# One half of a modulation bank computed at a layer boundary instead of inside the layer before, with a scratch tile and a modulation step rearranged

## The chip, the cores and the metric

The kernel runs on one core of a Trainium2 chip. The metric is the device time of one execution in microseconds (us); lower is better. Three runs of the kernel before gave 1622.14, 1630.13 and 1632.17 us, with a median of 1630.13 us.

## The reference, cut to what matters

The program is a trunk of two layers over 256 context and 256 latent tokens of width 1024, followed by a final norm. Each layer has six modulation vectors, each 1024 wide, worked out from a conditioning vector:

```python
mod = silu(c) @ w_ada[l] + b_ada[l]        # 6 x 1024 columns, mods 0 to 5
h   = rms_norm(x, norm1[l]) * (1 + scale) + shift
x   = x + gate * w_out(merge(conv(h), retention(h), mla(h)))   # one in-projection for the three
h2  = rms_norm(x, norm2[l]) * (1 + scale2) + shift2
x   = x + gate2 * moe(h2)                  # 16 experts, top 2 in groups
```

Everything is float32. The kernel stores the modulations in three banks of 2048 columns: bank 0 holds mods 0 and 1 (shift and scale of the first norm), bank 1 mods 2 and 3, bank 2 mods 4 and 5. In bank 1 of layer 1, mod 2 is the gate after the mixers and mod 3 the shift of the second norm.

## The kernel before, in words

**Numbers.** A float32 operand is split into a rounded part and a rest (`hi`, `lo`), and a product is three matmuls: hi by hi, lo by hi, hi by lo. In the trace the rounded weight is `whi` or `ehi` (made by ACT), its rest `wlo` or `elo` (made by DVE, L383 and L1095). The three matmuls are lines L185 to L187 in the projections, L192, L193 and L195 in the experts, and L1472, L1473 and L1475 in the last quarters of the last expert.

**Modulation banks (class `Ada`, L233).** A bank is computed in eight k-steps of 128 rows of `w_ada`. A step (L276) multiplies `silu(c)` by four column groups of 512 and sends the result of group g to partitions 32g to 32g+31 of one PSUM tile, `psa`. `add` (L287) adds the bias, and `finish` writes the bank to DRAM, from where `mod_row` reads it as rows. In layer 0 the banks (0,1), (0,2), (1,0) and (1,1), written as (layer, bank), stand in the list `todo`. `fill` takes one step of it behind a projection of layer 0, and `load` brings the step's weights, 128x2048 or 1 MB, into the single buffer `adaw`. Bank (1,2) is read through the stream of expert weights and multiplied where PE waits for the router, around 620 us.

**Expert weights.** `pieces` lists all weight pieces of a layer's experts, 512 KB each. `prefetch` (L1058) starts the load of the next piece on SP's queue as soon as a buffer is offered; `weights` (L1081) takes the next piece, makes `ehi` and `elo`, and gives the buffer back; `raw_piece` (L1075) does the same without making them. So a load that reuses a buffer waits for the last reader of the piece in it.

**The boundary.** `last_expert` (L1477) runs expert 15 of layer 0: its up projections (`ps<-ehi,xh` and so on), its transposed activations (L1444), its gate product `gg` (L1453), its down projection, first into the two tiles `py`, then in four quarters of 256 columns into `ps`. In `add`, PE scatters the result back to the tokens (L1491, `ps<-yg,ohT`), DVE multiplies it by a gate into `eth` (L1503) and adds that to `resid` (L1505), and ACT squares the new `resid` into a scratch tile, also a buffer of the tag `eth` (L1507), summing the squares. From these sums DVE makes the norm's factor (L201 to L209) and the normed rows `xn` (L564) of layer 1. Before these quarters stands a branch (L1562) on a flag that tells of overflowing experts; it isn't taken here, but every engine passes it.

Layer 1 then transposes `xn` (PE, L571), modulates it (`modulate`, L419: DVE makes `t` with scale and shift, L424; ACT rounds it to `hh`, L427; DVE makes `hl`, L428) and starts its in-projection (L185) while the rest is modulated.

**Order.** The order of the source is not the order of the engines: the framework's scheduler places each instruction in its engine's queue, and each queue then runs in order. `tc.issue_after` holds an instruction behind another one.

The lines that the change and the steps of the prediction touch:

Of the kernel before, what the change touches and what calls it, by code (L numbers as in the profile page):

```python
# [10 lines left out]
F32 = mybir.dt.float32  # L11
# [97 lines left out]
def tile_hybrid(ctx, tc, x, c, ctxt, c_ctx, w_ada, b_ada, norm1, norm2, w_in, ret_decay, ret_gn, w_ret_o,  # L109
# [18 lines left out]
    def nm(s):  # L128
        uid[0] += 1
        return f"{s}_{uid[0]}"  # L130
# [102 lines left out]
    class Ada:  # L233

        def __init__(self, l, b, pool, bufs, tps, alloc):
            self.l, self.b, self.pool, self.bufs, self.tps, self.alloc = l, b, pool, bufs, tps, alloc
            self.ps = None
            self.w = {}  # L240
            self.loaded = {}

        def prep(self):
            l, b = self.l, self.b
            self.bias = [self.alloc() for _ in range(1 if b == 1 else 2)]
            for t in self.bias:
                G.memset(t, 0.0)
            for g in range(4):
                r = b_ada[l, b * 2048 + g * 512:b * 2048 + (g + 1) * 512]
                nc.gpsimd.dma_start(self.bias[0][32 * g:32 * g + 2, :], r.partition_broadcast(2))  # L250
            if b != 1:
                nw = norm1 if b == 0 else norm2
                for g in range(2):
                    q = 32 * g + (64 if b == 0 else 0)
                    nc.gpsimd.dma_start(self.bias[1][q:q + 2, :], nw[l, g * 512:(g + 1) * 512].partition_broadcast(2))
            if b == 2 and self.pool is not None:
                G.tensor_scalar(self.bias[1], self.bias[1], ROW_SCALE, None, op0=ALU.mult)

        def load(self, k):
            l, b = self.l, self.b  # L260
            w = self.pool.tile([P, 2048], F32, name=nm("adaw"), tag="adaw", bufs=self.bufs)
            self.loaded[k] = nc.sync.dma_start(w, w_ada[l, k * P:(k + 1) * P, b * 2048:(b + 1) * 2048]).ins
            self.w[k] = w

        def step(self, k):
            l, b = self.l, self.b
            if k == 5 and self.pool is not None:
                self.prep()
            if k == 0:
                self.ps = psa.tile([P, 512], F32, name=nm("psa"), tag="psa")  # L270
            if k not in self.w:
                self.load(k)
            w = self.w.pop(k)
            for g in range(4):
                wg = w[:, g * 512:(g + 1) * 512] if not isinstance(w, list) else w[g // 2][:, g % 2 * 512:g % 2 * 512 + 512]
                self.last = TE.matmul(self.ps[32 * g:32 * g + 32, :], sC[:, k, :], wg, start=(k == 0), stop=(k == KD - 1)).ins  # L276
            if k == KD - 1 and self.pool is not None:
                self.add()

        def add(self):  # L280
            m, b = self.bias[0], self.b
            V.tensor_tensor(m, self.ps, m, op=ALU.add)
            if b != 1:
                q = slice(64, 128) if b == 0 else slice(0, 64)
                V.scalar_tensor_tensor(m[q, :], m[q, :], 1.0, self.bias[1][q, :], op0=ALU.add, op1=ALU.mult)

        def finish(self):  # L287
# [8 lines left out]
                    for kk in range(2):  # L296
                        V.tensor_copy(mfeat[:, l, n, 4 * kk:4 * kk + 4, :], tv[:, :, 2 * n + kk, 0:2])
            else:
                for g in range(4):
                    nc.gpsimd.dma_start(modd[l][:, b * 2048 + g * 512:b * 2048 + (g + 1) * 512],  # L300
                                        m[32 * g:32 * g + 2, :])

# [26 lines left out]
    for l in range(DEPTH):  # L329
# [89 lines left out]
        def modulate(src, k, s, n=1):  # L419

            hf = t2()
            hv = hf[:, :n * L].rearrange("p (a n) -> p a n", n=L)
            for a in range(n):
                V.tensor_scalar(hv[:, a, :], src[:, a, :], mfeat[:, l, 1, k + a, s:s + 1],  # L424
                                mfeat[:, l, 0, k + a, s:s + 1], op0=ALU.mult, op1=ALU.add)
            ks, cs = slice(k, k + n), slice(s * L, s * L + L)
            rounded.append(A.copy(hh[:, ks, cs], hv).ins)  # L427
            modulated.append(V.tensor_tensor(hl[:, ks, cs], hv, hh[:, ks, cs].bitcast(F32), op=ALU.subtract).ins)  # L428
# [4 lines left out]
        if l == 0:  # L433
# [111 lines left out]
            stA = ExitStack()  # L545
            ma = stA.enter_context(pool(f"mb{l}", side="right"))
            for al, ab_ in ((0, 1), (0, 2), (1, 0), (1, 1)):
                a = Ada(al, ab_, mx, 1, ps_tile, t2)
                todo += [(a, k) for k in range(KD + 1)]
        else:  # L550

# [21 lines left out]
                    yield  # L573


            for tg, n, b in (("pe", 512, 3), ("sc", 4 * L, 2), ("vv", 2048, 1), ("u", 516, 1), ("bh", 1536, 1)):
                ma.tile([P, n], F32, name=nm("first"), tag=tg, bufs=b)
            lows = []
            for c0 in (C_PC, C_PX, C_PB):
                early[c0] = load(w_in[l, :, c0:c0 + P], KD, P, behind=lows)  # L580
# [2 lines left out]

            order = [C_PC, C_PX, C_PB]
            pss = [ps_tile() for _ in order]
            with tc.issue_after(lows.pop(0)()):
                for n in range(KD // 2 + 2):
                    next(latents, None)
                    if lows:
                        with tc.issue_after(modulated[-1]):  # L590
                            lows.pop(0)()
                    for i, c0 in enumerate(order):
                        if 0 <= n - i < KD // 2:
                            for k in (2 * (n - i), 2 * (n - i) + 1):
                                wp = early[c0]
                                done = mm3(pss[i][:, :NQ], (wp[0][:, k, :], wp[1][:, k, :]),
                                           (hh[:, k, q0:], hl[:, k, q0:]), k == 0, k == KD - 1)
                            begun[c0] = pss[i], done
            context = (None for _ in ())

        def proj_g(c0, n=P, t0=q0, t1=NTOK):
# [66 lines left out]
        for j in range(4):  # L668
# [19 lines left out]
            pb = proj(C_PB + j * P)  # L688
            V.tensor_tensor(y[:, :NQ], y[:, :NQ], pb[:, :NQ], op=ALU.mult)
            if l > 0 and j == 0:  # L690

                with tc.issue_after(wdma[2]):
                    m5 = mod_row(ma, 0, 5, 0, "sc", 2)
# [348 lines left out]
            pieces += downs + ups if e < NE - 1 else ups + downs  # L1042

        pieces += [(w2[l, NE - 1, :, 256 * i:256 * i + 256], 4) for i in range(4)]
        raws = {}
        loaded = [0]
        used = [0]
# [73 lines left out]
        fill(100)  # L1121
        stH.close()
        mg = stM.enter_context(pool(f"mg{l}", side="right"))
        offer(NB, lambda: mg.tile([P, 1024], F32, name=nm("eraw"), tag="eraw2", bufs=NB))
        prefetch()


# [256 lines left out]
        for i in range(4):  # L1384
            offer(1, lambda i=i: zz[:, i, :], FOR[l] + n_ada)
        if l == 0:
            offer(ND[l], lambda: et("eraw3", [P, 1024], F32, ND[l]))
            offer(1, lambda: et("fx", [P, 1024]), REST[l] + n_ada)
            prefetch(most=6)
            with queued(h2w[-1]):  # L1390
# [86 lines left out]
        def last_expert(wps, yps, yg, ys, parts_):  # L1477
# [6 lines left out]
            def add(i):  # L1484
# [8 lines left out]
                for t in range(2):  # L1493

                    both = n == 256
                    if t == 0 or not both:
# [6 lines left out]
                            V.tensor_tensor(f_, f, m5, op=ALU.mult)  # L1503
                            f = f_
                        V.tensor_tensor(r, r, f, op=ALU.add)  # L1505
                    sq = et("eth", [P, 512], bufs=2)
                    A.activation(sq[:, :n], resid[:, 2 + t, cs], AF.Square, accum_out=ssq[:, t, i:i + 1])  # L1507

            for i, (cs, ps) in enumerate(cuts):
# [107 lines left out]
        if l == 0:  # L1617
# [223 lines left out]
            follow(True)  # L1841
            rs1 = run(last_expert(wps, None, ygs[1], ys[:cap], [(ohT[NE - 2 + i][:cap], ygs[i]) for i in range(2)]))
            nc.scalar.dma_start(yd[1 + (NE - 1) * cap:1 + NE * cap, :], ys[:cap, :])
        else:

            posn, keep, posm = slots_ = [sm(tg, NG) for tg in ("posn", "keep", "posm")]
# [168 lines left out]
```

## Time and profile before

| quantity | value |
|---|---|
| median of 3 runs | 1630.13 us |
| profiled execution, whole | 1623.87 us |
| its span in the profile | 1622.1 us |
| mean granted clock of TensorE in it | 0.978 |
| PE busy | 1532.8 us, 94% of the span |
| DVE busy | 1161.8 us, 72% |
| ACT busy | 847.0 us, 52% |
| POOL busy | 84.8 us, 5% |

PE is TensorE's matmuls, DVE VectorE, ACT ScalarE, POOL GpSimd, and SP the engine whose queue starts the weight loads. PE is the busiest engine, so time is won or lost where PE stands still or runs at a lower clock. A granted clock of 1.00 is 2.4 GHz and one of 0.50 is 1.2 GHz. The profiled execution is 6.3 us faster than the median of the three runs.

### The profile page before, as it was taken

How to read it: one execution, taken by the hardware profiler on the slowest of the kernel's cores; microseconds unless marked ns; L12 is line 12 of the kernel's file. 1: busy time of each engine (PE TensorE's matmuls, PEld its weight loads, DVE VectorE, ACT ScalarE, POOL GpSimd, SP SyncE). 2: the span in 40 equal slices, each digit the busy share in tenths (PEclk: the TensorE clock that was granted, in tenths of full speed). 3: DMA queues.
4: the chain of work that ended last, by engine and by line, in shares of the span. 5: the costliest groups of instructions: out<-in, count | busy, mean ns of one | idle time of the engine just before them, and what ended most of it. 6: DMA issues, size and time to landing. Idle time of an engine off the chain costs nothing. (4 is left out here: it accounts for less than half of the span.)

```text
span 1622.1 us, 21790 instructions
## 1 busy us (share of the span) xinstructions
PE 1532.8 (94%) x7811; PEld 1191.1 (73%) x7811; DVE 1161.8 (72%) x1978; ACT 847.0 (52%) x1218; POOL 84.8 (5%) x137
## 2 busy tenths in 40 slices
PE   4999999999999997999999969999999989999996
PEld 1766776667767884777777759888978868888775
DVE  3633376426674457899999989577676699999897
ACT  3512233334442223688788845346454467777674
POOL 1011010000000004200000210000000000000000
PEclk8999999999999998999999979999999989999998
DMA  9676354643117448999999956335436579999981
GB/s 343 190 237 227 98 169 139 192 130 105 40 53 257 164 173 300 336 376 364 377 384 373 370 172 182 104 105 150 132 90 208 180 263 371 347 390 326 361 304 64
DMA packets 238281, 370.94 MB, mean 229 GB/s; under 512 B 16147, under 2 KB 133365, under 8 KB 233045
## 3 DMA queue, kind: packets, MB, share of 16 engines
q1 hardware_dynamic: 228944, 345.06, 62.7%
q0 software_dynamic: 6400, 15.13, 3.2%
q10 hardware_dynamic: 2820, 9.28, 1.5%
q8 instruction: 64, 1.05, 0.3%
q14 instruction: 53, 0.43, 0.1%
HBM read 357.69 MB, written 11.73 MB: 228 GB/s over the span
## 5 line engine op out<-in xcount | busy, mean ns | idle before, releaser
L1095 DVE TENSOR_TENSOR elo<-eraw,ehi 128x1024 fp32r<-128x1024 f32 x291 | 344.5, 1218 | 10.3 <-ACT ehi L1093 7.9
L1093 ACT CAST ehi<-eraw 128x1024 fp32r<-128x1024 f32 x291 | 301.2, 1050 | 72.8 <-PE ps L193 44.4
L383 DVE TENSOR_TENSOR wlo<-wraw,whi 128x1024 fp32r<-128x1024 f32 (+1 forms) x146 | 176.4, 1210 | 190.0 <-ACT whi L375 187.8
L375 ACT CAST whi<-wraw 128x1024 fp32r<-128x1024 f32 (+1 forms) x146 | 151.2, 1038 | 275.3 <-PE ps L186 181.6
L185 PE MATMUL ps<-hh,whi 128*128 128x512 f32 (+1 forms) x800 | 286.8, 360 | 4.1 <-ACT hh L427 1.8
L186 PE MATMUL ps<-hl,whi 128*128 128x512 f32 (+1 forms) x800 | 276.5, 346 | 0.1
L187 PE MATMUL ps<-hh,wlo 128*128 128x512 f32 (+1 forms) x800 | 274.9, 345 | 0.3 <-DVE wlo L383 0.3
L185 PEld LDWEIGHTS ps<-hh,whi 128*128 128x128 f32 x800 | 151.1, 189 | 41.9 <-issue 16.5
L186 PEld LDWEIGHTS ps<-hl,whi 128*128 128x128 f32 x800 | 151.2, 189 | 27.8 <-issue 9.5
L187 PEld LDWEIGHTS ps<-hh,wlo 128*128 128x128 f32 x800 | 150.8, 189 | 23.3 <-issue 3.6
L192 PE MATMUL ps<-ehi,xh 128*112 128x512 f32 x256 | 104.0, 406 | 3.9 <-ACT xh L225 3.9
L193 PE MATMUL ps<-ehi,xl 128*112 128x512 f32 x256 | 103.5, 404 | 0.7 <-DVE xl L226 0.6
L192 PE MATMUL ps<-ehi,xgh 128*128 128x512 f32 x256 | 102.3, 400 | 0.2 <-ACT ehi L1093 0.2
L193 PE MATMUL ps<-ehi,xgl 128*128 128x512 f32 x256 | 101.3, 396 | 0.0
L192 PE MATMUL py<-ehi,gg 128*112 128x512 f32 (+1 forms) x240 | 93.6, 391 | 1.8 <-PEq L1562 1.6
L193 PE MATMUL py<-ehi,gg 128*112 128x512 f32 (+1 forms) x240 | 93.1, 390 | 0.0
L1095 DVE TENSOR_TENSOR elo<-raws,ehi 128x1024 fp32r<-128x1024 f32 x72 | 86.0, 1218 | 4.9 <-ACT ehi L1093 2.2
L1093 ACT CAST ehi<-raws 128x1024 fp32r<-128x1024 f32 x72 | 74.7, 1050 | 19.7 <-PE ps L193 11.0
L195 PE MATMUL ps<-elo,xgh 128*128 128x512 f32 x256 | 80.8, 396 | 1.2 <-DVE elo L1095 1.1
L195 PE MATMUL ps<-elo,xh 128*112 128x512 f32 x256 | 80.8, 397 | 0.6 <-DVE elo L1095 0.6
L195 PE MATMUL py<-elo,gg 128*112 128x512 f32 (+1 forms) x240 | 74.7, 393 | 1.5 <-DVE elo L1095 1.4
L959 ACT ACTIVATE pe<-ps,mxv 128x512 f32<-128x512 f32 (+1 forms) x48 | 29.6, 617 | 62.1 <-DVE mxv L957 58.4
(473 smaller groups left out, 2762.9 us busy)
## 6 DMA issues: line engine op xcount, KB each, us to landing
eraw<-in_w_dram SPq DMA_DIRECT2D x291, 512.0 KB
wraw<-in_w_in_dram SPq DMA_DIRECT2D x106, 512.0 KB
adaw<-in_w_ada_dram SPq DMA_DIRECT2D x40, 1024.0 KB
raws<-in_w_dram SPq DMA_DIRECT2D x72, 512.0 KB
wraw<-in_w_out_dram SPq DMA_DIRECT2D x16, 512.0 KB
wraw<-in_w_dram SPq DMA_DIRECT2D x15, 512.0 KB
yd<-ys ACTq DMA_DIRECT2D x16, 448.0 KB
eraw<-in_w_ada_dram SPq DMA_DIRECT2D x13, 512.0 KB
```

What stands on the lines that cost most here:

```text
L185: TE.matmul(ps, wp[0], xp[0], start=first, stop=False)
L186: TE.matmul(ps, wp[0], xp[1], start=False, stop=False)
L187: return TE.matmul(ps, wp[1], xp[0], start=False, stop=last).ins
L192: TE.matmul(ps, x_[0], w_[0], start=first, stop=False)
L193: TE.matmul(ps, x_[1], w_[0], start=False, stop=False)
L195: ins = TE.matmul(ps, x_[0], w_[1], start=False, stop=last)
L375: his.append(A.copy(hi[:, :kt * n], raw[:, :kt * n]).ins)
L383: return V.tensor_tensor(lo[:, :kt * n], raw[:, :kt * n], hi[:, :kt * n].bitcast(F32), op=ALU.subtract).ins
L959: A.activation(pe[:, :nk], sps[:, :nk], AF.Exp, scale=MLA_SCALE, bias=mxv[:, 1:2], accum_out=mxv[:, 2:3])
L1093: latest["hi"] = A.copy(hi, raw).ins
L1095: latest["lo"] = V.tensor_tensor(lo, raw, hi.bitcast(F32), op=ALU.subtract).ins
```

## The change

Five edits are made. First, bank (1,1) is cut in two. Its half 0 (mod 2) stays in `todo` and now has two column groups per step, with a load of 128x1024. Its half 1 (mod 3) becomes eight more pieces behind the last expert piece of layer 0 (`n_exp` is the number of pieces before them); its eight steps, `gap_ada`, are written behind `last_expert`. Its bias is loaded at the start of layer 1, and its `add` and `finish` stand in layer 1's conv loop. Second, ACT's squares in layer 0's `last_expert` get a scratch tile of their own, `late`. Third, of the two column tiles that `modulate` handles in one call, the second is made by ACT instead of DVE. Fourth, the first loop of layer 1's in-projection is no longer held behind its first `wlo`. Fifth, two more tiles are reserved at the start of layer 1, and two groups of buffers are offered only up to piece `n_exp`.

```diff
-        def __init__(self, l, b, pool, bufs, tps, alloc):
+        def __init__(self, l, b, pool, bufs, tps, alloc, half=None):
+            self.groups = range(4) if half is None else range(2 * half, 2 * half + 2)
+            self.rows = slice(32 * self.groups[0], 32 * self.groups[-1] + 32)
...
-            self.loaded[k] = nc.sync.dma_start(w, w_ada[l, k * P:(k + 1) * P, b * 2048:(b + 1) * 2048]).ins
+            cs = slice(self.groups[0] * 512, self.groups[-1] * 512 + 512)
+            self.loaded[k] = nc.sync.dma_start(w[:, cs], w_ada[l, k * P:(k + 1) * P,
+                                                               b * 2048 + cs.start:b * 2048 + cs.stop]).ins
...
-            for g in range(4):
+            for g in self.groups:
                 wg = w[:, g * 512:(g + 1) * 512] if not isinstance(w, list) else w[g // 2][:, g % 2 * 512:g % 2 * 512 + 512]
...
-                V.tensor_scalar(hv[:, a, :], src[:, a, :], mfeat[:, l, 1, k + a, s:s + 1],
-                                mfeat[:, l, 0, k + a, s:s + 1], op0=ALU.mult, op1=ALU.add)
+                scale, shift = (mfeat[:, l, i, k + a, s:s + 1] for i in (1, 0))
+                if a:
+                    A.activation(hv[:, a, :], src[:, a, :], AF.Identity, scale=scale, bias=shift)
+                else:
+                    V.tensor_scalar(hv[:, a, :], src[:, a, :], scale, shift, op0=ALU.mult, op1=ALU.add)
...
-                a = Ada(al, ab_, mx, 1, ps_tile, t2)
+                a = Ada(al, ab_, mx, 1, ps_tile, t2, 0 if (al, ab_) == (1, 1) else None)
...
+            gap_ada.alloc = lambda: ma.tile([P, 512], F32, name=nm("gapb"), tag="pe", bufs=3)
+            gap_ada.prep()
...
-            with tc.issue_after(lows.pop(0)()):
-                for n in range(KD // 2 + 2):
+            for n in range(KD // 2 + 2):
...
             if l > 0 and j == 0:
+                with tc.issue_after(gated[0]):
+                    gap_ada.add()
+                gap_ada.finish()
...
+        n_exp = len(pieces)
+        if l == 0:
+            pieces += [(w_ada[1, kk * P:(kk + 1) * P, 3072:4096], 1) for kk in range(KD)]
...
-                    sq = et("eth", [P, 512], bufs=2)
+                    sq = et("late", [P, 512]) if l == 0 else et("eth", [P, 512], bufs=2)
...
             rs1 = run(last_expert(wps, None, ygs[1], ys[:cap], [(ohT[NE - 2 + i][:cap], ygs[i]) for i in range(2)]))
             nc.scalar.dma_start(yd[1 + (NE - 1) * cap:1 + NE * cap, :], ys[:cap, :])
+            gap_ada = Ada(1, 1, None, 0, None, None, 1)
+            for kk in range(KD):
+                gap_ada.w[kk] = [None, raw_piece()]
+                gap_ada.step(kk)
```

The order of the engines differs at the boundary. In the rows below a tile has its buffer number, and the changed kernel's lines are some 10 to 18 higher: a step of a bank is L281 (before L276), the branch L1580 (before L1562), the quarters L1490 and L1491 (before L1472 and L1473).

PE, in the up projections of expert 15 of layer 0, before:

```order
L192 MATMUL ps_1628_7680<-ehi_1633_7703,xh_1607_7593 112x512
L193 MATMUL ps_1628_7680<-ehi_1633_7703,xl_1608_7594 112x512
L195 MATMUL ps_1628_7680<-elo_1634_7704,xh_1607_7593 112x512 x2
L192 MATMUL ps_1628_7680<-ehi_1635_7714,xh_1607_7593 112x512
L193 MATMUL ps_1628_7680<-ehi_1635_7714,xl_1608_7594 112x512
L192 MATMUL ps_1628_7680<-ehi_1635_7714,xh_1607_7593 112x512
L193 MATMUL ps_1628_7680<-ehi_1635_7714,xl_1608_7594 112x512
L195 MATMUL ps_1628_7680<-elo_1636_7715,xh_1607_7593 112x512 x2
L1444 MATMUL ps_1645_7753<-cst_58,eth_1637_7725 128x112 x4
```

PE at the same place in the changed kernel:

```order
L192 MATMUL ps_1631_7666<-ehi_1636_7689,xh_1607_7573 112x512
L193 MATMUL ps_1631_7666<-ehi_1636_7689,xl_1608_7574 112x512
L281 MATMUL psa_1725_8236<-eraw_1621_7622,sC_61 32x512 x2
L281 MATMUL psa_1725_8236<-eraw_1625_7638,sC_61 32x512 x2
L195 MATMUL ps_1631_7666<-elo_1637_7690,xh_1607_7573 112x512 x2
L192 MATMUL ps_1631_7666<-ehi_1638_7700,xh_1607_7573 112x512
L193 MATMUL ps_1631_7666<-ehi_1638_7700,xl_1608_7574 112x512
L192 MATMUL ps_1631_7666<-ehi_1638_7700,xh_1607_7573 112x512
L193 MATMUL ps_1631_7666<-ehi_1638_7700,xl_1608_7574 112x512
L281 MATMUL psa_1725_8236<-eraw_1629_7654,sC_61 32x512 x2
L195 MATMUL ps_1631_7666<-elo_1639_7701,xh_1607_7573 112x512 x2
L1462 MATMUL ps_1648_7739<-cst_58,eth_1640_7711 128x112 x4
```

Three of the eight steps now stand inside the up projections of expert 15, ahead of work that doesn't need them.

PE just ahead of the branch in the changed kernel; before, the branch followed the matmuls of `elo` that stand here two pieces earlier, and the pieces `ehi_1650` and `ehi_1653` came behind it:

```order
L192 MATMUL py_1642_7717<-ehi_1653_7759,gg_1618_7615 112x512
L193 MATMUL py_1642_7717<-ehi_1653_7759,gg_1618_7615 112x512
L192 MATMUL py_1643_7718<-ehi_1653_7759,gg_1618_7615 112x512
L193 MATMUL py_1643_7718<-ehi_1653_7759,gg_1618_7615 112x512
L195 MATMUL py_1642_7717<-elo_1654_7760,gg_1618_7615 112x512
L195 MATMUL py_1643_7718<-elo_1654_7760,gg_1618_7615 112x512
L281 MATMUL psa_1725_8236<-eraw_1652_7751,sC_61 32x512 x2
L281 MATMUL psa_1725_8236<-eraw_1657_7773,sC_61 32x512 x2
L281 MATMUL psa_1725_8236<-eraw_1660_7779,sC_61 32x512 x2
L281 MATMUL psa_1725_8236<-eraw_1663_7785,sC_61 32x512 x2
L1580 COMPARE_AND_BRANCH
```

Four more steps have come to stand between the down projection and the branch; one, of the piece `eraw_1666`, stands behind PE's last scatter.

SP's queue at the boundary in the changed kernel, from the last load of an expert's weights on:

```order
L1084 DMA eraw_1615_7598<-in_w2_dram 128x4x256
L1084 DMA eraw_1621_7622<-in_w_ada_dram 128x1024
L1084 DMA eraw_1625_7638<-in_w_ada_dram 128x1024
L1084 DMA eraw_1629_7654<-in_w_ada_dram 128x1024
L1084 DMA eraw_1657_7773<-in_w_ada_dram 128x1024
L1084 DMA eraw_1660_7779<-in_w_ada_dram 128x1024
L1084 DMA eraw_1663_7785<-in_w_ada_dram 128x1024
L1084 DMA eraw_1652_7751<-in_w_ada_dram 128x1024
L1084 DMA eraw_1666_7791<-in_w_ada_dram 128x1024
L1580 COMPARE_AND_BRANCH
```

Before, the branch stood right behind the first of these. The loads 7773, 7779 and 7785 reuse the buffers of 7622, 7638 and 7654 and wait for their steps; 7751 waits for DVE's `elo_1651_7748` and 7791 for `elo_1656_7770`.

ACT at the start of layer 1 in the changed kernel (L381 is the rounding of a projection's weights, L436 that of `hh`):

```order
L381 CAST whi_1736_8285<-wraw_1735_8284 128x1024
L432 ACTIVATE t2_1749_8310<-ps_1748_8305,mfeat_65 128x256
L381 CAST whi_1739_8290<-wraw_1738_8289 128x1024
L436 CAST hh1_8271<-t2_1749_8310 128x2x256
L381 CAST whi_1742_8295<-wraw_1741_8294 128x1024
L432 ACTIVATE t2_1751_8327<-ps_1750_8322,mfeat_65 128x256
```

Before, the three casts of `whi` stood together ahead of the first `hh`; now one of them stands between the first tile's modulation and its rounding.

## Rows read from the trace of the kernel before

**Rows 1.** Stretches: busy of PE, PEld, DVE, ACT, POOL; granted clock, DMA share, GB/s.

```profile
930.00:935.00 5.00, 5.00 (x23) 3.58 (x22) 5.00 (x6) 3.11 (x4) 0.00 (x0) 1.00 1.06 366
...
960.00:965.00 5.00, 0.00 (x0) 0.00 (x0) 3.90 (x20) 3.85 (x9) 1.93 (x2) 0.52 0.82 235
...
970.00:975.00 5.00, 5.00 (x28) 4.78 (x27) 3.04 (x6) 0.62 (x1) 1.81 (x1) 0.61 0.97 193
```

**Rows 2.** PE in order of time from 934 us: start, length, in brackets the wait.

```profile
934.10 0.69 PE L195 MATMUL ps<-elo,xh 128*112 128x512 f32 x2
...
936.35 0.72 PE L195 MATMUL ps<-elo,xh 128*112 128x512 f32 x2 [0.63 <-DVE elo L1095]
939.01 0.60 PE L1444 MATMUL ps<-cst,eth 112*128 112x112 f32 x4 [1.93 <-DVE eth L1435]
940.14 1.19 PE L195 MATMUL py<-elo,gg 128*112 128x512 f32 x2 [0.53 <-DVE elo L1095]
...
945.23 0.46 PE L192 MATMUL py<-ehi,gg 128*112 128x512 f32 x1 [1.60 <-PEq L1562]
```

**Rows 3.** PE in order of time from 957 us.

```profile
957.66 0.86 PE L1491 MATMUL ps<-yg,ohT 112*128 112x256 f32 x5 [0.33 <-DVE yg L226]
965.30 1.47 PE L571 MATMUL ps<-cst,xn 128*128 128x128 f32 x4 [6.78 <-DVE xn L564]
968.55 0.58 PE L185 MATMUL ps<-hh,whi 128*128 128x256 f32 x1 [1.79 <-ACT hh L427]
```

**Rows 4.** Steps of banks: source line L276 from 290 to 375 us.

```profile
L276 PE MATMUL psa<-adaw,sC x64: 592/605/617, 294.7 to 371.6; 128*32 128x512 f32 x64
...
  DMA adaw<-in_w_ada_dram: 4.5, 2
```

**Rows 5.** The same steps and bank (1,2)'s on PE, in order of time.

```profile
355.18 1.07 PE L276 MATMUL psa<-adaw,sC 128*32 128x512 f32 x8
...
621.65 5.34 PE L276 MATMUL psa<-eraw,sC 128*32 128x512 f32 x32
```

**Rows 6.** The same columns in stretches of 1 us, where layer 0's weight stream ends.

```profile
935.00:936.00 1.00, 0.72 (x4) 0.21 (x2) 1.00 (x2) 0.35 (x1) 0.00 (x0) 1.00 0.76 239
936.00:937.00 1.00, 0.65 (x2) 0.27 (x2) 1.00 (x2) 0.63 (x1) 0.00 (x0) 1.00 0.58 188
937.00:938.00 1.00, 0.07 (x1) 0.00 (x0) 1.00 (x3) 0.43 (x1) 0.00 (x0) 1.00 0.23 77
...
940.00:941.00 1.00, 0.86 (x2) 0.74 (x3) 1.00 (x2) 1.00 (x2) 0.00 (x0) 0.50 0.65 154
...
942.00:943.00 1.00, 1.00 (x4) 0.75 (x3) 0.89 (x1) 0.00 (x0) 0.00 (x0) 0.50 0.21 55
```

**Rows 7.** SP's queue: expert pieces from 895 us, and layer 1's first weights.

```profile
L1066 SPq DMA_DIRECT2D eraw<-in_w_dram x18: 327/379/4313, 895.0 to 929.7; - x18
938.84 11.40 SPq L372 DMA_DIRECT2D wraw<-in_w_in_dram  x3
```

**Rows 8.** DVE in order of time, expert 15 and the last additions.

```profile
938.22 0.73 DVE L1435 SCALAR_TENSOR_TENSOR eth<-eth,gtab,ps 112x512 f32<-112x512 f32 x1
938.88 2.35 DVE L1095 TENSOR_TENSOR elo<-eraw,ehi 128x1024 fp32r<-128x1024 f32 x2
...
941.68 4.85 DVE L1095 TENSOR_TENSOR elo<-eraw,ehi 128x1024 fp32r<-128x1024 f32 x4
...
955.86 0.69 DVE L1503 TENSOR_TENSOR eth<-ps,mr 128x512 f32<-128x512 f32 x1 [0.58 <-ACT eth L1507]
...
957.91 0.69 DVE L1503 TENSOR_TENSOR eth<-ps,mr 128x512 f32<-128x512 f32 x1 [0.30 <-ACT eth L1507]
...
959.90 0.69 DVE L1503 TENSOR_TENSOR eth<-ps,mr 128x512 f32<-128x512 f32 x1 [0.57 <-ACT eth L1507]
```

**Rows 9.** ACT and DVE at layer 1's first modulation.

```profile
962.22 2.92 ACT L375 CAST whi<-wraw 128x1024 fp32r<-128x1024 f32 x3
...
966.87 0.98 DVE L424 TENSOR_SCALAR t<-ps,mfeat 128x256 f32<-128x256 f32 x2
```

More of the change, by code (lines that the diff above doesn't have):

```diff
@@ L273, in step @@
             w = self.w.pop(k)
-            for g in range(4):
+            for g in self.groups:
                 wg = w[:, g * 512:(g + 1) * 512] if not isinstance(w, list) else w[g // 2][:, g % 2 * 512:g % 2 * 512 + 512]
@@ L281, in add @@
             m, b = self.bias[0], self.b
-            V.tensor_tensor(m, self.ps, m, op=ALU.add)
+            q = self.rows
+            V.tensor_tensor(m[q, :], self.ps[q, :], m[q, :], op=ALU.add)
             if b != 1:
@@ L298, in finish @@
             else:
-                for g in range(4):
+                for g in self.groups:
                     nc.gpsimd.dma_start(modd[l][:, b * 2048 + g * 512:b * 2048 + (g + 1) * 512],
@@ L573, in norm1_g @@
                     yield
-            for tg, n, b in (("pe", 512, 3), ("sc", 4 * L, 2), ("vv", 2048, 1), ("u", 516, 1), ("bh", 1536, 1)):
+            for tg, n, b in (("pe", 512, 3), ("sc", 4 * L, 2), ("vv", 2048, 1), ("u", 516, 1), ("bh", 1536, 1),
+                             ("bl", 1536, 1), ("kt", 2048, 1)):
                 ma.tile([P, n], F32, name=nm("first"), tag=tg, bufs=b)
+            gap_ada.alloc = lambda: ma.tile([P, 512], F32, name=nm("gapb"), tag="pe", bufs=3)
+            gap_ada.prep()
             lows = []
@@ L585, in tile_hybrid @@
             pss = [ps_tile() for _ in order]
-            with tc.issue_after(lows.pop(0)()):
-                for n in range(KD // 2 + 2):
[L588 to L598, printed above, removed]
+            for n in range(KD // 2 + 2):
+                next(latents, None)
+                if lows:
+                    with tc.issue_after(modulated[-1]):
+                        lows.pop(0)()
+                for i, c0 in enumerate(order):
+                    if 0 <= n - i < KD // 2:
+                        for k in (2 * (n - i), 2 * (n - i) + 1):
+                            wp = early[c0]
+                            done = mm3(pss[i][:, :NQ], (wp[0][:, k, :], wp[1][:, k, :]),
+                                       (hh[:, k, q0:], hl[:, k, q0:]), k == 0, k == KD - 1)
+                        begun[c0] = pss[i], done
             context = (None for _ in ())
@@ L1123, in tile_hybrid @@
         mg = stM.enter_context(pool(f"mg{l}", side="right"))
-        offer(NB, lambda: mg.tile([P, 1024], F32, name=nm("eraw"), tag="eraw2", bufs=NB))
+        offer(NB, lambda: mg.tile([P, 1024], F32, name=nm("eraw"), tag="eraw2", bufs=NB), n_exp)
         prefetch()
@@ L1386, in tile_hybrid @@
         if l == 0:
-            offer(ND[l], lambda: et("eraw3", [P, 1024], F32, ND[l]))
+            offer(ND[l], lambda: et("eraw3", [P, 1024], F32, ND[l]), n_exp)
             offer(1, lambda: et("fx", [P, 1024]), REST[l] + n_ada)
```

## The prediction

> **What bounds the kernel now.** I read the page first: PE is busy for 94% of the span, so an edit counts only where PE stands still, runs at half clock, or gets or loses work. Next I read the stretches around the boundary of the layers [rows 1]: PE is fully busy until 935 us, does nothing from 960 to 965 us, and the granted clock there falls to 0.52 and is still 0.61 as a mean from 970 to 975 us. PE in order of time names the waits. The long one is 6.78 us, from the last scatter to layer 1's first transposes, ended by DVE's `xn` [rows 3]. Behind it come 1.79 us for ACT's `hh`. Ahead of it, in expert 15, PE waits 0.63, 1.93 and 0.53 us for DVE and 1.60 us at the branch [rows 2]. The reader should see two things here: a hole of 6.78 us that useful matmuls could fill, and a stretch ahead of it, from 934 to 945 us, where PE runs close behind DVE and whatever delays PE delays the chain to the end of the layer.
>
> **Layer 0: steps halved.** From 290 to 375 us the eight steps of bank (1,1) leave 64 records on PE, and PE waited twice for their weights, 4.5 us in all [rows 4]. Each load falls from 1024 to 512 KB. The weight stream moves 366 GB/s [rows 1], so 512 KB (0.524 MB) take 1.43 us at that rate, and the two waits shrink by up to 2 x 1.43 = 2.9 us. The PE time of a step is eight records in 1.07 us [rows 5]; as one record alone lasts 0.605 us [rows 4], the four column groups run side by side. Half a step may therefore cost anything from 0.5 us (half) to 1.0 us (nearly all) at full clock. So PE wins between 0 and 8 x 0.5 = 4 us here. I take 2 us for waits and work together; the bounds are 0 and 6.9 us.
>
> The Trainium skill ("TensorE: Matmul & The Clock Gate", section "Measured speedup vs the span model") speaks against halving: it measured 2.38 times the speed for three column tiles at once, so taking tiles away from such a pack saves little. By it I estimate that four tiles take about 1.3 times and two about 1.1 times one tile's time, so that a half step saves some 0.15 us, 1.2 us over eight; by a strict half it would be 4 us. The rows agree with the rule as far as the four groups overlap; none of them shows two groups alone.
>
> **The boundary: eight steps added.** They were written for the hole of 6.78 us, but the order shows only one of them there. Steps 0 and 1 stand ahead of the `elo` matmuls that ran at 934.10 us, step 2 ahead of those of 936.35 us, and four ahead of the branch. PE's queue runs in order, so if a step's weights are late, all behind it waits. The pieces come last in SP's queue. The last issue of an expert piece starts at 929.7 us [rows 7]. What still moved after 930 us was 5 x 366 = 1830 KB to 935 us [rows 1] and 239 + 188 + 77 = 504 KB to 938 us [rows 6], 2334 KB in all. Three more pieces of 524 KB at 366 KB per us land at about (2334 + 524) / 366 = 7.8 us behind 930 us, that is 937.8 us, then 939.2 and 940.7 us.
>
> PE comes to step 0 at 934.1 us and waits 3.7 us. I follow it with steps of 1.0 us and, in brackets, of 0.5 us. Step 0 ends at 938.8 (938.3), step 1 at 940.2 (939.7). Then follow the two `elo` matmuls and four more, 1.6 us at full clock (from 934.10 us to 936.35 less the wait of 0.63 us, 935.72 us, before [rows 2]); I allow 2.3 us with some of it at half clock in the first case, because the clock read 0.50 at 940 us after the wait of 1.93 us [rows 2, 6]. Step 2 ends at 943.5 (941.8), and the last `elo` matmuls at 944.2 (942.5). Before, they ended at 937.1 us, and DVE took its next input, L1435, at 938.22 us [rows 8], 1.1 us later, because it was busy with other work; that work is done by now. L1435 therefore shifts by 6.0 (4.3) us.
>
> DVE is in order too: two `elo`, the gate product `gg` and four more `elo` stood behind L1435 [rows 8] and all shift with it. That puts the `elo` of the third piece of the down projection, whose buffer the load 7751 wants, at 942.9 + 6.0 = 948.9 (947.2) us. A single load took from its issue at 938.84 us to about 942.3 us [rows 6, 7], 3.4 us, so piece 7751 lands at 952.3 (950.6) us. PE waits for it with the down projection finished, makes four steps until 956.3 (952.6) us, and passes the branch in 1.6 us, at 957.9 (954.2) us. Before, it stood there at 945.23 us and took until 958.52 us, the end of the last scatter [rows 3]; 2.6 us of this were the twelve `py` matmuls of two pieces, at 0.22 us each (23 in 5.00 us [rows 1]), which now come earlier. The 10.7 us left end at 968.6 (964.9) us, that is 10.1 (6.4) us later than before. I take 8 us, about the middle, as no row shows half a step.
>
> **Scratch of their own.** DVE waited 0.58, 0.30 and 0.57 us for ACT's squares in the shared buffers [rows 8]: 1.45 us on the chain that ends in `xn`. With the tile `late` these waits go. What is late next is PE's scatter itself, 0.3 us away, so I take 1.2 us; the bounds are 0 and 1.45 us.
>
> **Modulation on two engines.** The two halves of a tile took DVE 0.98 us, 0.49 us each [rows 9]. Now ACT makes one, but into the same tile, and in the built program ACT waits for DVE's half; side by side they would save 0.5 us. ACT's queue also has a cast of `whi` between its half and `hh`; three of these took 2.92 us [rows 9], so 1.0 us more before PE's first product. I take a loss of 0.5 us, bounds -0.5 and +1.1 us. Step 7 runs inside the hole at no cost, and `add`, the bias and the writes to DRAM aren't needed until layer 1's conv loop is over, when DVE and POOL have gaps. The clock stays half after a hole that is still over 5 us long: 0, at best 2 us won. The dropped hold on the first loop and the limits on buffers move nothing in the order: 0.
>
> **Sum.** Against the profiled execution: 1623.87 - 2 + 8 - 1.2 + 0.5 = 1629.2 us, 5.3 us more. The profiled execution lies 6.3 us below the median of the runs, 1630.13 us, so I forecast 1630.13 + 5.3 = 1635.4, rounded to 1635 us. The ends of the terms are -6.9 + 6.4 - 1.45 - 0.5 - 2 = -4.5 us and 0 + 10.1 - 0 + 1.1 = +11.2 us, 1626 to 1641 us.
>
> **The rivals.** First: the steps fill the waits. The order differs only at two places, and if the pieces land two or three us sooner (at 935 us the stream is already thinning [rows 6]), seven steps of 0.5 us, 3.5 us, fit into the 0.63 + 1.93 + 0.53 + 1.60 = 4.69 us that PE waits there anyway [rows 2]. Then layer 0's 2 us, up to 2 us more there, and the 1.2 us of the scratch stay: 3 to 5 us faster, about 1626 us. Against it speaks that the pieces queue behind 2334 KB, and that piece 7751 can't be issued before DVE is done with its buffer.
>
> Second, on the slower side: the late load of piece 7751 decides. The SP queue passes its branch only when all of its loads have landed, the last of them, 7791, as well, and layer 1's first three weights (issued from 938.84 us before [rows 7]) come behind it. If the clock is half throughout, each step costs 2 us in place of 1, seven steps 7 us more; layer 1's weights, one load behind the other, are then up to 3 us late for the first products. On the forecast's 5.3 us that gives about 15 us, 1645 us. It decides if 7751 lands after about 955 us. For it speaks the clock of 0.50 after a wait of only 1.93 us; against it, that layer 1's weights had over 10 us to spare.
>
> Third: the change is neutral. The modulation runs one half after the other, the hole is as long as before, and what layer 0 gives is what the boundary takes: 1630 us. The last scatter would have to shift by less than 4 us, which needs pieces that land by 936 us.
>
> **How the numbers follow.** Forecast 0.5, the first rival 0.2, the second 0.15, the third 0.15. The range goes from the forecast's own 1626 to 1641 us out to most of the outer cases, and adds that three runs of one kernel spread over 10 us: 1618 to 1647 us. A measurement tells 1%, 16.3 us, from no change: below 1613.8 us is faster, above 1646.4 us is slower. No case reaches the first bound, which leaves 0.03 for what I don't see; of the second rival a third lies beyond the other, 0.05.
>
> **What would show it.** In the trace of the changed kernel: PE waits of 3 to 4 us for a load of `eraw` inside expert 15's up projections, and again ahead of the branch; L1491's last scatter ends around 966 us instead of 958.5; DVE's waits before L1503 are gone; the hole before L571 is between 5 and 6 us; the steps around 300 to 370 us wait less for `adaw`. The forecast is wrong if PE waits less than 1 us for the first of these pieces, if the last scatter comes within 3 us of its old time, or if the modulations of the two engines overlap and the clock is back by 970 us.

## The result, and the profile after

The changed kernel took 1638.36 us (median of 12 runs, 1633.81 to 1641.18), the kernel before 1626.45 us (12 runs, 1622.14 to 1632.17). The ratio is 1.0065, with a 95% interval of 1.0054 to 1.0076: slower by about two thirds of a per cent, 10.6 us of the 1630.13 us that the forecast started from. The forecast was 1635 us in a range of 1618 to 1647 us. The way was right, and so was the place; the size was about twice the 5.3 us of the sum. That the forecast still lies within 3.4 us of the measured time is partly luck: the 1630.13 us it started from, the median of three runs, lie 3.7 us above the median of twelve, and this made up for more than half of what the sum lacked. The profiled execution after has a span of 1636.6 us, 14.5 more than the one of before.

To see where the time went, I matched PE's matmuls of the two traces one by one and looked at how much later each starts.

| place (time before) | later by |
|---|---|
| 288 us, ahead of bank (1,1) in layer 0 | 3.73 us |
| 389 us, behind it | 1.68 us |
| 932 us, ahead of the first step in expert 15 | 1.24 us |
| 939.01 us, transposes of expert 15 (L1444) | 9.76 us |
| 958.52 us, end of the last scatter (L1491) | 12.58 us |
| 965.30 us, first transposes of layer 1 (L571) | 11.70 us |
| 968.55 us, first product of layer 1 (L185) | 12.66 us |
| 1003 us | 14.06 us |
| from 1026 us to the end | 14.4 to 14.5 us |

The first row isn't the change's: no instruction ahead of it is altered, and in the traces of the experiments below the same place lies anywhere from 0.2 us earlier to 4.3 us later. The halved steps give 2.05 us back. Another 0.4 us goes between 620 and 720 us, a stretch that the change doesn't touch either and that differs from trace to trace. The stretch from 932 to 1026 us costs 13.2 us, and nothing is won or lost behind it.

PE in order of time in the changed kernel, from 941 us; these rows answer to [rows 2, 3]:

```profile
941.42 3.31 PE L281 MATMUL psa<-eraw,sC 128*32 128x512 f32 x8 [5.91 <-DMA eraw<-in_w_ada_dram]
...
946.23 1.05 PE L281 MATMUL psa<-eraw,sC 128*32 128x512 f32 x4
...
948.77 0.60 PE L1462 MATMUL ps<-cst,eth 112*128 112x112 f32 x4 [0.84 <-DVE eth L1453]
...
956.60 3.63 PE L281 MATMUL psa<-eraw,sC 128*32 128x512 f32 x16 [1.79 <-DMA eraw<-in_w_ada_dram]
961.44 0.34 PE L1490 MATMUL ps<-ehi,gg 128*112 128x256 f32 x1 [1.21 <-PEq L1580]
...
969.04 2.06 PE L1509 MATMUL ps<-yg,ohT 112*128 112x256 f32 x16
971.03 1.05 PE L281 MATMUL psa<-eraw,sC 128*32 128x512 f32 x4
977.00 0.45 PE L580 MATMUL ps<-cst,xn 128*128 128x128 f32 x1 [4.92 <-DVE xn L573]
...
981.21 0.58 PE L185 MATMUL ps<-hh,whi 128*128 128x256 f32 x1 [2.69 <-ACT hh L436]
```

The reader should see the two waits for `eraw`, 5.91 and 1.79 us, and that behind each of them PE makes steps which nothing needed yet. The two steps of the first row run at half clock: eight records in 3.31 us, where four take 1.05 us at 946.23 and 971.03 us. The hole is now 4.92 us with one step in front of it; PE's wait for `hh` has grown from 1.79 to 2.69 us.

The second of these two steps also meets its piece only on arrival. PE's weight loads (PEld) in order of time:

```profile
942.69 0.14 PEld L281 LDWEIGHTS psa<-eraw,sC 128*32 128x32 f32 x2 [1.08 <-DMA eraw<-in_w_ada_dram]
```

No view prints the moments of landing themselves, but the trace keeps 16 landing events for each of these loads, and a load is complete with the last of them. The last expert piece lands at 940.11 us and the first three pieces of the bank at 941.38, 942.65 and 943.91 us: one behind the other, 1.27 us apart. In the kernel before, the last expert piece landed at 938.62 us.

Stretches of 1 us of the changed kernel (busy time of PE, PEld, DVE, ACT and POOL, then granted clock, DMA share and GB/s), which answer to [rows 6]:

```profile
936.00:937.00 1.00, 0.00 (x0) 0.00 (x0) 1.00 (x2) 0.59 (x1) 0.00 (x0) 1.00 1.08 372
...
938.00:939.00 1.00, 0.00 (x0) 0.00 (x0) 1.00 (x2) 0.00 (x0) 0.00 (x0) 0.50 1.05 415
...
940.00:941.00 1.00, 0.00 (x0) 0.00 (x0) 0.00 (x0) 0.00 (x0) 0.00 (x0) 0.50 0.59 238
941.00:942.00 1.00, 0.58 (x2) 0.19 (x4) 0.00 (x0) 0.00 (x0) 0.00 (x0) 0.50 0.16 61
```

The weight stream, which thinned out at 935 us before, runs full until 940 us and then thins out; step 0 starts as its piece is complete. From 940 to 942 us neither DVE nor ACT has anything to do: both wait for PE.

DVE in order of time in the changed kernel, the rows that answer to [rows 8], and the addition of the bank in layer 1:

```profile
947.97 0.75 DVE L1453 SCALAR_TENSOR_TENSOR eth<-eth,gtab,ps 112x512 f32<-112x512 f32 x1 [8.42 <-PE ps L195]
...
970.19 0.69 DVE L1521 TENSOR_TENSOR eth<-ps,mr 128x512 f32<-128x512 f32 x1
...
971.52 0.68 DVE L1521 TENSOR_TENSOR eth<-ps,mr 128x512 f32<-128x512 f32 x1
...
996.24 0.69 DVE L288 TENSOR_TENSOR gapb<-psa,gapb 64x512 f32<-64x512 f32 x1
```

DVE, which had no wait in front of this row before [rows 8], stands 8.42 us for PE. The last two multiplications of the scatter's results no longer wait for ACT's squares, so the scratch of their own does what it says.

### The profile page after: what moved, and what is told of

Read it like the earlier page. It is cut to its first block, busy times and chain, and to the rows that moved or that the text cites. A ratio compares the mean times of both kernels' runs of the same rounds, so it can differ in the third digit from the quotient of the medians.

```text
span 1636.6 us, 21811 instructions
## 1 busy us (share of the span) xinstructions
PE 1539.3 (94%) x7811; PEld 1191.1 (73%) x7811; DVE 1159.4 (71%) x1971; ACT 852.0 (52%) x1226; POOL 82.9 (5%) x138
## 3 DMA queue, kind: packets, MB, share of 16 engines
q8 instruction: 64, 1.05, 0.3%
## 5 line engine op out<-in xcount | busy, mean ns | idle before, releaser
L381 ACT CAST whi<-wraw 128x1024 fp32r<-128x1024 f32 (+1 forms) x146 | 151.5, 1039 | 276.2 <-PE ps L186 192.7
L185 PE MATMUL ps<-hh,whi 128*128 128x512 f32 (+1 forms) x800 | 287.7, 360 | 5.0 <-ACT hh L436 2.7
L185 PEld LDWEIGHTS ps<-hh,whi 128*128 128x128 f32 x800 | 151.3, 189 | 43.1 <-issue 16.5
```

The costliest lines, as they stand in the source:

```text
L185: TE.matmul(ps, wp[0], xp[0], start=first, stop=False)
L381: his.append(A.copy(hi[:, :kt * n], raw[:, :kt * n]).ins)
```

## The experiments

All were timed in rounds against the kernel before, whose median was 1625.9 to 1626.6 us in these comparisons.

**The squares' scratch alone (e1_scratch).** In the kernel before:

```diff
-                    sq = et("eth", [P, 512], bufs=2)
+                    sq = et("late", [P, 512]) if l == 0 else et("eth", [P, 512], bufs=2)
```

> Only the squares' scratch of the change, in the kernel before. Theory (the waits of 0.58, 0.30 and 0.57 us before L1503 go and the chain to xn is shorter): 1.2 to 1.7 us less than before, the hole before L571 near 5.3 us in place of 6.78. Rival (PE's scatter sets the chain anyway): no change of the hole, 0 us.

Measured: 1624.66 us against 1626.59, ratio 0.999 (0.998 to 0.9999), about 1.6 us less. PE in order of time of this run, at layer 1's first transposes:

```profile
963.16 0.45 PE L571 MATMUL ps<-cst,xn 128*128 128x128 f32 x1 [5.88 <-DVE xn L564]
```

The hole is 5.88 us in place of 6.78 [rows 3], 0.9 us less, where a hole near 5.3 us was expected. DVE's waits in front of L1503 for ACT are gone, but the sum of the squares still waits 1.18 us for ACT's last square, as it waited 1.03 us before. This part of the change is a gain, but one that the timing only just tells from nothing (its interval is 0.2 to 3.3 us), so its size is known only roughly.

**The modulation on two engines alone (e2_modulate).** In the kernel before, the second column tile of `modulate` made by ACT as in the change.

> Only the modulation on two engines, in the kernel before. Theory (the two halves run one after the other, because both write one tile, and a cast of whi comes between): the wait of PE for the first hh grows from 1.79 to about 2.7 us, 1 to 1.6 us more in all. Rival (two engines share the work): the wait shrinks to about 1.3 us and the time falls by 0.5 to 2 us.

Measured: 1627.94 us against 1626.59, ratio 1.0016 (1.0007 to 1.0026): 1.4 us more by the medians, 2.6 by the ratio, with 1.1 to 4.2 us in the interval. ACT in order of time of this run, at the first tile of layer 1:

```profile
968.01 0.56 ACT L426 ACTIVATE t<-ps,mfeat 128x256 f32<-128x256 f32 x1 [3.24 <-DVE t L428]
968.48 1.03 ACT L375 CAST whi<-wraw 128x1024 fp32r<-128x1024 f32 x1
969.41 0.62 ACT L430 CAST hh<-t 128x512 fp32r<-128x512 f32 x1
```

ACT starts its half when DVE's is done, and a cast of `whi` stands between it and `hh`. PE waited 2.73 us for this `hh`. Two engines that write one tile one after the other are slower here than one.

**The halved steps in layer 0 alone (e3_half).** The kernel before, with two column groups per step of bank (1,1). This leaves out the half of the bank that holds mod 3.

> The kernel before with steps of two column groups for bank (1,1) in layer 0; the other half of the bank (mod 3) isn't computed, so its bias alone is used. Theory (half a step costs PE nearly a whole one, and only the waits for adaw shrink): 2 us less than before, the offset between 290 and 375 us. Rival (half a step costs half): 4 us of PE time and 2 us of waits, 5 to 6 us less.

Measured: 1624.67 us against 1626.59, ratio 0.9992 (0.9982 to 1.0003), which the timing doesn't tell from no change. The trace does: between 288 and 389 us PE's matmuls gain 2.1 us. PE in order of time of this run, one step and what follows:

```profile
295.10 1.05 PE L280 MATMUL psa<-adaw,sC 128*32 128x512 f32 x4
296.08 0.50 PE L185 MATMUL ps<-hh,whi 128*128 128x512 f32 x1
```

In the kernel before, PE's waits from 288 to 389 us had this line, which is gone in this run:

```profile
PE psa L276 <- DMA adaw<-in_w_ada_dram: 1.9, 1, 1.9
```

Four records take 1.05 us where eight took 1.07 [rows 5], so half a step frees almost no PE time, 0.02 us. The gain is the wait for `adaw`: PE itself waited once, 1.9 us. The 4.5 us in two waits of [rows 4] count this one load twice, once for PE's matmul and once for its weight load (2.5 us). The rival with half the cost falls.

The kernel before had shown this already. It makes one of its eight steps in two parts, of one and of three column groups (a group is two records), and each part takes as long as a whole step:

```profile
337.53 1.05 PE L276 MATMUL psa<-adaw,sC 128*32 128x512 f32 x2
...
348.71 1.06 PE L276 MATMUL psa<-adaw,sC 128*32 128x512 f32 x6
```

**All eight steps in the hole (e4_hole).** The changed kernel, loads behind the branch, steps held behind the last scatter. The buffers `eraw3`, which the change kept from the bank's pieces, are offered to them too, here and in the runs below that move the loads:

```diff
+        limit = [n_exp]
...
-            while free and loaded[0] < len(pieces) and most:
+            while free and loaded[0] < limit[0] and most:
...
                     beyond(flag, gov)
+                    limit[0] = len(pieces)
+                    prefetch()
...
-                gap_ada.step(kk)
+                with tc.issue_after(latest["scat"]):
+                    gap_ada.step(kk)
```

> The changed kernel with the eight loads issued behind the branch and the eight steps held behind PE's last scatter, all in the hole. Theory (the change lost its time because steps stood ahead of the branch and waited there for late weights): the waits of 5.91 and 1.79 us for eraw go and with them about 11 us; the steps take 8 x 0.98 = 7.8 us in a hole of 5.5 us, the clock stays full, the two other edits still cost 2 to 3 us: 1624 to 1629 us, against 1638 with the change. Rival (the traffic of the eight loads at the boundary, or the other edits, cost the time): it stays above 1633 us.

Measured: 1629.57 us, ratio 1.0022 (1.0013 to 1.0031) to the kernel before. Of the 11.9 us between the medians 8.9 go, of the 10.6 us by the ratios 7.0. PE in order of time of this run:

```profile
957.80 7.06 PE L281 MATMUL psa<-eraw,sC 128*32 128x512 f32 x32
965.72 0.33 PE L580 MATMUL ps<-cst,xn 128*128 128x128 f32 x1 [0.86 <-DVE xn L573]
966.52 0.55 PE L580 MATMUL ps<-cst,xn 128*128 128x128 f32 x3 [0.47 <-DVE xn L573]
969.76 0.58 PE L185 MATMUL ps<-hh,whi 128*128 128x256 f32 x1 [2.69 <-ACT hh L436]
```

The same 32 records, with the same bytes loaded at the same boundary, run without a wait in one block of 7.06 us. So neither the traffic nor the steps as such cost the most, but that they stood ahead of other work while their weights were still on the way. One expectation missed: the clock didn't stay full. It was 0.77 from 965 to 970 us, where PE is busy for 1.1 of 5 us, and 0.55 from 970 to 975 us.

**The loads behind the branch, the steps left free (e11_free).** As the run above, without the hold.

> The changed kernel with the eight loads behind the branch, as in the run with the steps in the hole (1629.6 us), but with the steps left where the scheduler puts them: four of them between the last quarters and scatters of expert 15. Theory (a step costs where it stands ahead of the scatter, and nothing in the hole): the last scatter comes 3 to 4 us later, 1 to 3 us more than 1629.6 us, still well under the change's 1638 since no step waits long for its weights. Rival (only the wait for weights costs, not the place): 1629.6 us or less.

Measured: 1631.06 us, ratio 1.0034 (1.0021 to 1.0046), 1.5 us above the steps in the hole by the medians. The two intervals overlap by a little, so the place between the scatters is not shown to cost much by the timing. In the two traces, counted from 932 us, the last scatter does end 3.5 us later than with the steps in the hole, as was expected, but layer 1's first transposes come only 1.0 us later. What is shown is that with no late weight the loss stays far under the change's 11.9 us. In its trace PE waits nowhere for `eraw`.

**The change with one edit undone (e7_add, e8_dve).** In the first, the bank's addition moved behind layer 1's conv loop; in the second, the modulation on DVE alone.

> The changed kernel with only the addition of the bank moved behind layer 1's conv loop. Theory (DVE is full from 996 to 1009 us, so the 0.69 us of the addition push PE by 0.8 and then 0.4 us): about 1.2 us less than the change, 1637 us. Rival (it is hidden): the same 1638.4 us.

> The changed kernel with only the modulation put back on DVE alone. Theory: the wait for the first hh falls from 2.69 to about 1.8 us, 1 to 2 us less than the change, 1636.5 to 1637.5 us. Rival (the late weights ahead of the branch hide what ACT does): the same 1638.4 us.

Measured: 1637.46 us (ratio 1.0066, 1.0052 to 1.0081) and 1636.41 us (1.0071, 1.0055 to 1.0087). Both intervals hold the change's own 1.0065, so the timing can't settle either. The traces tell more. PE's wait for `wlo` in order of time, in the changed kernel:

```profile
1006.36 0.39 PE L187 MATMUL ps<-hh,wlo 128*128 128x256 f32 x1 [1.07 <-DVE wlo L389]
```

and in the run with the addition moved:

```profile
1005.76 0.39 PE L187 MATMUL ps<-hh,wlo 128*128 128x256 f32 x1 [0.17 <-DVE wlo L389]
```

From the end of the last scatter to 1040 us the changed kernel falls behind by another 1.9 us, the run with the addition moved by 0.5 us and the one with the modulation undone by 0.4 us. In the second, PE's wait for `hh` is 1.74 us again.

**Both undone, with the steps in the hole (e6_hole_dve).**

> The run with all eight half steps in the hole, with the modulation on DVE alone again and the addition of the bank moved behind layer 1's conv loop. Theory (these two edits cost 0.9 us at the first hh, and 0.8 and 0.4 us at two later waits for DVE): 2 to 3 us less than the 1629.6 us of that run, 1626 to 1628 us. Rival (the eight steps themselves cost the time there): 1629 us or more.

Measured: 1625.67 us, ratio 0.9997 (0.9987 to 1.0007): the expected gain of 2 to 3 us came in full (3.2 us by the two distances to the kernel before, 4.1 by the ratios). With its steps in the hole and these two edits undone the change is neutral: in its trace layer 0 gives 2.0 us, and the stretch from 932 to 1026 us, own scratch included, costs 2.1 us.

**Cut by rows (e5_rows).** Four whole steps stay in layer 0 and four go into the hole:

```diff
-            self.groups = range(4) if half is None else range(2 * half, 2 * half + 2)
+            self.groups, self.half = range(4), half
+            self.k0, self.k1 = (0, KD) if half is None else (half * (KD // 2), (half + 1) * (KD // 2))
...
+                if self.half == 1:
+                    r = modd[l][:, b * 2048 + g * 512:b * 2048 + (g + 1) * 512]
...
-            pieces += [(w_ada[1, kk * P:(kk + 1) * P, 3072:4096], 1) for kk in range(KD)]
+            pieces += [(w_ada[1, kk * P:(kk + 1) * P, 2048 + 1024 * h:3072 + 1024 * h], 1) for kk in range(KD // 2, KD) for h in range(2)]
```

> The bank is cut by rows instead of columns: four whole steps of four column groups (k 0 to 3) stay in layer 0, their sum goes to DRAM, and four whole steps (k 4 to 7) are made in the hole on top of it, loaded behind the branch and held behind PE's last scatter; own scratch kept; modulation on DVE alone as before; the addition of the bank moved to where DVE has time. Theory (a step costs PE about 1.0 us however many groups it has, so only whole steps taken away free PE time): 4 us of PE time and about 2 us of waits leave layer 0, the four steps fit into the hole, the scratch gives up to 2 us: 1617 to 1622 us. Rival (what leaves layer 0 comes back at the boundary, in loads that delay layer 1's weights): not under 1624 us.

Measured: 1624.34 us, ratio 0.9992 (0.9981 to 1.0004), short of the 1617 to 1622 us. The time alone would fit the rival as well, but the wait that the trace names is another one. The trace shows layer 0 giving 6.7 us, as hoped, and PE losing 5.1 us in one wait for DVE's `wlo` at 989 us. POOL in order of time of this run:

```profile
958.74 0.98 POOL L323 DMA_INDIRECT f<-yd,ii  x1 [4.23 <-issue]
959.72 2.14 POOL L256 DMA_DIRECT2D gapb<-modd  x4
964.65 2.18 POOL L323 DMA_INDIRECT f<-yd,ii  x1 [2.80 <-DMA f<-yd,ii]
967.14 1.91 POOL L323 DMA_INDIRECT f<-yd,ii  x1 [0.30 <-issue]
975.49 2.64 POOL L323 DMA_INDIRECT f<-yd,ii  x1 [6.44 <-DMA f<-yd,ii]
```

The four small loads of the partial sums stand between the first gather of the expert rows and the rest, and the last gather, which itself waits 6.44 us for the landing of another, starts at 975.49 us, where the kernel before started it at 969.66 us. DVE's addition of these rows waits, and `wlo` waits behind it. DVE in order of time of this run:

```profile
984.70 1.22 DVE L328 TENSOR_TENSOR f<-f,mr 128x1024 f32<-128x1024 f32 x1 [4.61 <-DMA f<-yd,ii]
```

**The same with these loads behind the gathers (e9_rows_late, e10_columns_late).** Rows and columns, each with DVE's modulation and the late addition:

```diff
-            gap_ada.prep()
             lows = []
...
+            with tc.issue_after(gathers[-1]):
+                gap_ada.prep()
```

> The bank cut by rows as in the run before, with the loads that the addition needs (gapb) moved on POOL behind the gathers of the expert rows. Theory (those four loads stood between the gathers, the fourth gather came 6 us late, and through DVE's add PE waited 5.1 us for wlo): the wait goes, about 5 us less than 1624.3 us, 1617 to 1621 us, clearly faster than before. Rival (layer 1's weights come late because the eight loads go ahead of them): the wait for wlo stays, 1623 us or more.

> The bank cut by columns, all eight half steps in the hole, modulation on DVE, addition late, with the same move of gapb's loads behind the gathers. Theory (half steps free almost no PE time in layer 0 and take 7 us in the hole, whole ones free 4 us and take 3.6): 1624 to 1626 us, 5 us or more above the cut by rows. Rival (the cut doesn't matter, only the place in the queues): within 2 us of the cut by rows.

Measured: by rows 1620.52 us, ratio 0.9964 (0.9951 to 0.9978); by columns 1626.57 us, ratio 1.0002 (0.9993 to 1.0011). The cut by rows is 6 us faster than the cut by columns and beats both the kernel before and the change. PE in order of time of the run by rows,

```profile
950.21 2.78 PE L284 MATMUL psa<-eraw,sC 128*32 128x512 f32 x24
953.93 1.05 PE L284 MATMUL psa<-eraw,sC 128*32 128x512 f32 x4 [0.94 <-DMA eraw<-in_w_ada_dram]
956.39 1.05 PE L284 MATMUL psa<-eraw,sC 128*32 128x512 f32 x4 [1.41 <-DMA eraw<-in_w_ada_dram]
958.30 0.33 PE L581 MATMUL ps<-cst,xn 128*128 128x128 f32 x1 [0.86 <-DVE xn L574]
```

and DVE's normed rows in the same run:

```profile
957.50 1.44 DVE L574 TENSOR_SCALAR xn<-resid,ss 128x1024 f32<-128x1024 f32 x2 [2.19 <-PE psa L284]
```

The last pieces come late here too, by 0.94 and 1.41 us, and even the hole isn't free: `xn` waits 2.19 us for PE's last step, though it reads nothing of it. The transposes come 8.0 us behind the end of the last scatter at 950.3 us, against 6.78 us before [rows 3]. (With the half steps in the hole, e4_hole, `xn` waited 2.01 us in the same way.) That `xn` reuses the memory of a piece would explain it, but was not tested; it leaves some 2 us to be won. That most of the wait of 5.1 us was POOL's doing is shown: with these loads behind the gathers the last gather starts at 966.96 us, DVE no longer waits for it, and the wait for `wlo` at that place is 1.96 us. The kernel before waited 0.27 us there; what the rest is due to was not tested.

## Why the prediction was right, and where it was off

**The way and the mechanism: right.** The text said that three steps inside the up projections and four ahead of the branch would wait for weights that come last in SP's queue. They did, for 5.91 and 1.79 us (6.31 and 1.81 us in e7_add, 6.20 and 1.76 us in e8_dve), and taking the steps out of that place took 8.9 of the 11.9 us away (e4_hole).

**Layer 0, 2 us: right in size, partly by luck.** The gain in the trace is 2.05 us. The text took waits and work together and named 4.5 us of waits, of which 2.9 could go, and up to 4 us of work. PE's own wait was 1.9 us, all of it went, and the work gave almost nothing (e3_half). The text's range from 0.5 to 1.0 us for half a step could have been closed beforehand, by the row at 337.53 us. On the work the Trainium skill ("TensorE: Matmul & The Clock Gate", section "Measured speedup vs the span model") had the right sign: by the estimate drawn from it a half step would save 0.15 us, by a strict half 0.5 us, and the runs show 0.02 us.

**The boundary, 8 us (6.4 to 10.1): too small.** The last scatter ends 12.58 - 1.24 = 11.3 us later. The step of the working that failed is the landing of the pieces "at about 937.8 us, then 939.2 and 940.7 us". That they land one behind the other was right; that the first is there at 937.8 us was not. It was complete at 941.38 us, 940.1 us on the old time, 2.3 us later, and the two others came 1.27 us apart behind it. The sum divided all bytes that still moved by the full rate of 366 GB/s. But in the kernel before, the last expert piece, which stands ahead of the bank's pieces in the queue, landed at 938.62 us itself, later than the sum has the piece behind it. In the changed kernel 15 of the 16 parts of the first piece were there at 939.63 us, 938.4 us on the old time, and the last one came 1.75 us behind them; why that part lags is open. PE stood 5.91 us, not 3.7. The clock fell to 0.50 in this stand, and from 941.42 us the two steps took 3.24 us until the next matmul, not 2.4; the matmuls behind them, with the clock on its way back (0.86 from 944 us, 1.00 from 945 us), took 1.6 us and not the 2.3 allowed for. DVE's L1435 shifted by 947.97 - 938.22 - 1.24 = 8.5 us, not 4.3 to 6.0. The late load of piece 7751 was foreseen rightly: PE waited 1.79 us for it.

**The scratch, 1.2 us: right as far as can be told** (0.9 us of the hole in the trace, about 1.6 us in the timing, alone). **The modulation, a loss of 0.5 us: too small.** Alone it costs 1.4 to 2.6 us. The reason was the right one, the shared tile and the cast in between; but the text left out that the first `hh` is followed by others, and in the changed kernel PE falls from 11.70 to 13.26 us behind, 1.6 us, from the first transposes to 985 us.

**The addition, nothing: wrong.** The text named DVE's gaps behind the conv loop as its cover, but the addition stands inside the loop, at 996.24 us, where DVE has none, and PE pays 0.8 us at 1006.36 us and 0.4 us at the next `xn`. That cover was assumed and not looked up.

**The sum.** The measured terms, -2.05 + 11.3 - 0.9 for the hole (the scratch and step 7 inside it) + 1.6 for the modulation + 1.2 for the addition, make 11.2 us, which agrees with 11.9 us between the medians and 10.6 by the ratio. They are read from one trace of each kernel; in the trace of e3_half, which alters nothing there, the stretch from 932 us to the last scatter is also 1.5 us longer than before, so a term of about 1 us is uncertain by itself. Of the rivals, the first (the steps fill the waits) and the third (neutral) fall. The second had half its case: the clock fell and two steps took longer, but it was the first piece that decided and not 7751, and PE's first product of layer 1 waited for `hh` and not for its weights.

Why the scheduler put the steps ahead of the branch was not tested. The body of the branch, which isn't run here, uses buffers of the same tags as the pieces, and the code asks for them behind the loads; that would make the scheduler empty these buffers first. In the runs that issue the loads behind the branch the steps stand behind it, which fits, but this remains an argument.

## What to carry to other kernels

Work that is written behind a stage runs where the scheduler puts it; read the order of the engine before costing it, and look for each moved step's weights in the queue that loads them. A piece that is loaded last should be consumed where the engine would idle anyway, and not ahead of work that others wait for; and what follows the idle place must not wait for it, as `xn` did here for 2 us. To take work away from an engine, find what its price goes by: here a step costs the same with one, two or four column groups, so cutting by rows gave 6 us that cutting by columns didn't. And to say when a queued load lands, look at when the load ahead of it lands; bytes divided by the full rate came out 2.3 us too early here.

## What the runs showed of the hardware that was not expected

The first of three loads of 512 KB, issued on SP's queue behind a stream of about 370 GB/s, was complete 9.0 us after its issue (932.42 to 941.38 us), and the three landed 1.27 us apart; the load of piece 7751, issued into a nearly idle stream, took 3.9 us (952.71 to 956.56 us). Of the 16 parts of each load at the end of the full stream, the last came 1.8 us behind the other fifteen in the profiled execution of the changed kernel and 0.1 to 0.3 us behind them in that of the kernel before; the cause is open. A step of two column groups took PE 1.05 us, one of four 1.07 us, and one group alone 1.05 us. And four small loads, 2.14 us on POOL's queue between gathers, went with a last gather that started 8.5 us later than without them there (975.49 against 966.96 us) and a wait of PE of 5.1 us in place of 2.0.
